# Input projections of a hybrid decoder layer: TensorE in written order, the forget gates one product on, x in natural order

## The chip, the cores and the metric

The kernel runs on one core of a Trainium2 chip (trn2). The metric is the device time of one execution in microseconds. A core has five engines with instruction streams of their own: TensorE (PE in the profile; PEld is its weight load), VectorE (DVE), ScalarE (ACT), GpSimd (POOL) and SyncE (SP). Each works through its stream in order, and they wait for each other by semaphores. SP and ACT also issue transfers (their DMA queues). TensorE writes to PSUM, which the other engines must empty before a bank can be written again.

## The reference

One layer of a causal decoder over S = 2048 tokens of D = 1024 channels, in float32:

```python
nx = rmsnorm(h, attn_norm_g[l])
proj = jnp.einsum('bsd,dp->bsp', nx, w_in[l])
gq, gk, gv, gr, glow, dq, dk_, dv_ = jnp.split(proj, split_at, axis=-1)

gate_pre = (jnp.einsum('bsr,rk->bsk', glow, gla_gate_w2[l]) + gla_gate_b[l]).astype(jnp.float32)
glog = jax.nn.log_sigmoid(gate_pre) / GLA_TAU
o_a = gla_mixer(gq, gk, gv, glog)                  # reshaped per head
...
o_b = dilated_mixer(dq, dk_, dv_, rel_bias)        # reshaped per head
...
h = h + jnp.einsum('bsm,md->bsd', mixed, w_out[l])
nm = rmsnorm(h, mlp_norm_g[l])
a = jnp.square(jax.nn.relu(jnp.einsum('bsd,df->bsf', nm, w_ff1[l])))
h = h + jnp.einsum('bsf,fd->bsd', a, w_ff2[l])
```

The case is about the first lines: the norm of x, the projection `nx @ w_in` (1024 to 3088 columns), the forget gate made from the 16 low-rank columns `glow`, and the tables of the relative-position bias that the dilated attention reads later.

## The kernel before

**Products.** Every float32 matrix product is made of three matmuls on split operands (`mm3`, L67 to L69): high part by high part, low by high, high by low. On top of this the projection uses a scheme with seven products instead of eight for each block of 2 by 2: the 1024 tokens of a half in two blocks, channels in two blocks, a group's columns in two blocks. The seven sums of the x blocks, transposed so that channels lie on the partitions, are kept in the tiles `tb1` to `tb7` (high and low); the seven sums of the weight blocks are made as they are needed by `prep(at)` (L202 to L214) out of `wraw` into a ring of three `wcomb` tiles, two jobs ahead.

**Groups and jobs.** The columns of `w_in` are cut into nine groups, in this order: dv, gr, four of dq and dk, gq, gk, gv. Each is done for the first 1024 tokens and then again for the second, which makes 18 groups; each group has seven jobs, one for each of the seven products, in the order 1, 2, 5, 6, 3, 4, 7. So there are 126 jobs, numbered from 0. A job of a wide group (dv, gr, gv: two blocks of 256 or 264 columns) consists of four products, one for each tile of 128 tokens, `product(at, i)`; a job of a narrow group is one product with 512 tokens as the moving side. Each product is twelve matmuls into one PSUM bank. The banks come from rings with the tags a (2 banks), c (3), d (2) and o (1); products take them in the turn a, c, a, o. Behind each product `rest()` moves it out of PSUM and into the sums of its group, on ACT, DVE and POOL (L300 to L321), and `finish` stores columns that are done.

**The gates.** The group gr holds the output gate (248 or 264 columns a block) and, at the end of its second block, the 16 columns `glow`. The second column block is finished, for both token blocks, by the seventh product, so that the last job of the group (job 13 in the first token half, job 76 in the second) ends with eight gates, two behind each of its four products: for the two token tiles t that the product completes. There `rest()` runs L317 (DVE, out of PSUM), L318 (POOL) and L319 (DVE), and then `finish` twice. For gr, `finish` takes the log-sigmoid (`log_sigmoid`, L125 to L128: Abs, Exp and Ln on ACT, one DVE instruction), an Exp (L260), a DVE product (L261) and a POOL product (L262), stores the block, and calls `gate`. `gate` transposes glow (16 columns, L227) into a bank d, copies it to a small tile `gT` (L228), multiplies it by `w2b` into another bank d (L230), and runs the log-sigmoid on 256 columns straight from that bank.

**x.** `x_load` fetches a tile of 128 tokens by `token_rows`, in an order in which partition p holds token (p div 8) + 16 (p mod 8) of the tile, so that tokens 16 apart lie together. A tile is squared and summed on ACT (`x_stat`, L358), scaled by its inverse root and by the gain row `gB` (L370), which one transfer has spread over all partitions, and transposed by `transposed` (L378) with the identity. The first eight tiles are done in the opening, jobs 0 to 4, which is written out by hand. The other eight come from `second_half`, a generator that is advanced at the jobs listed in `OTHER`: load, norm (L420, L93, L94, L422), two times eight transposes, sums and stores to DRAM, from where `reload` brings them back for the second token half.

**Biases.** At job 65 `bias_rows` loads a table and makes three rows by three matmuls (L334) into the one o bank, with a DVE copy behind each (L335), and stores them to `rowD`. `spread_bias` then repeats each row over 128 partitions by a transfer from DRAM to DRAM on ACT's queue (L341): twelve of them, written at every third job from 72 to 105.

**What sets the order.** Within `tc.manual_schedule(engines=...)` the engines named keep the order in which the instructions are written. Outside, a scheduler at build time orders each engine's stream, by a model of its own and by the data that each instruction needs. Before, only the opening (jobs 0 to 4) is manual, for TensorE, DVE, ACT and POOL; SP's stream is the scheduler's throughout, and so is all of the loop over jobs 5 to 125. There the twelve bias transfers stand together on ACT's queue, soon after the rows, and the gates stand between the products of the following jobs.

Of the kernel before, what the change touches and what calls it, by code (L numbers as in the profile page):

```python
# [41 lines left out]
def emit(tc, a, stop=99):  # L42
# [35 lines left out]
    make_identity(nc, ident)  # L78
    mhalf = const.tile([128, 4], F32, name="mhalf")
    V.memset(mhalf, -0.5)  # L80
    stats = const.tile([128, 96], F32, name="stats")
    stat_at = [0]

    def stat(n=1):
        if stat_at[0] + n > 96:
            stat_at[0] = 0
        s = stats[:, stat_at[0]:stat_at[0] + n]
        stat_at[0] += n
        return s
# [132 lines left out]
    def gate(glow, t):  # L222

        gT = gTs[t % 2]
        V.memset(gT, 1.0)
        pt = ps("d")
        T.transpose(pt[:16, :128], glow, ident)  # L227
        V.tensor_copy(gT[:16], pt[:16, :128])  # L228
        pg = ps("d")[:, :256]
        T.matmul(pg, gT, w2b, start=True, stop=True)  # L230
        e = stage()[:, :256]
        log_sigmoid(e, pg)
        SP.dma_start(glD[t * 128:t * 128 + 128], e)
# [39 lines left out]
    banks = [0]  # L273

    def product(at, i):
# [11 lines left out]
        else:  # L287
            p = p[:, :w]
            tk = slice(i * 128, i * 128 + 128)
            for c in range(4):  # L290
                mm3(p, B[0][:, c, tk], B[1][:, c, tk], W[0][:, c], W[1][:, c], c == 0, c == 3)

# [32 lines left out]
    def bias_rows():  # L325
# [5 lines left out]
        SP.dma_start(oh, a["c_onehot"])  # L331
        for d in range(3):
            p = ps("o")
            T.matmul(p[:8, :384], rb, oh[:, d], start=True, stop=True)  # L334
            V.tensor_copy(rbo[:, d], p[:8, :384])  # L335
        SP.dma_start(rowD, rbo)

    def spread_bias(d, h):

        row = rowD[h:, d]  # L340
        A.dma_start(rbD[d][h:h + 2].rearrange("h p n -> p h n"),  # L341
                    bass.AP(tensor=row.tensor, offset=row.offset, ap=[[0, 128], [3 * 384, 2], [1, 384]]))
# [5 lines left out]
    def x_load(t, dst):  # L348
        SP.dma_start(dst, token_rows(x2, t, D))
# [22 lines left out]
    def transposed(xt, last=None):  # L372
        out = []
        for q in range(2):
            pv = view(ps("cd"[q]), (4, 128))
            for k in range(4):
                of = xt[:, (4 * q + k) * 128:(4 * q + k + 1) * 128]
                T.transpose(pv[:, k, :], last if last is not None and 4 * q + k == 7 else of, ident)  # L378
# [6 lines left out]
    def first_half(t):  # L385

        pv = transposed(xs[t])
# [22 lines left out]
    def second_half():  # L410

        b = [view(bp[:, 512 * q:], (4, 128)) for q in range(4)]
        for i in range(4):
# [10 lines left out]
            for k in range(2):  # L424
                for q, pv in enumerate(transposed(xp[:, D * k:])):
# [16 lines left out]
    with tc.manual_schedule(engines={nc.tensor.engine, nc.vector.engine, nc.scalar.engine, nc.gpsimd.engine}):  # L442
        x_load(0, xs[0])
        SP.dma_start(gB, bcast_row(a["attn_norm_g"], D))
# [55 lines left out]
    other, back = second_half(), []  # L500
    for at in range(5, len(jobs)):
# [13 lines left out]
        if at == 7 * NG + 2:  # L515
            bias_rows()
        if 7 * NG + 8 <= at < 7 * NG + 44 and at % 3 == 0:
            spread_bias(2 - (at - 7 * NG - 8) // 12, (at - 7 * NG - 8) // 3 % 4 * 2)
    if stop <= 1:
# [872 lines left out]
```

## Time and profile before

| what | value |
|---|---|
| median of three runs | 2397.13 us (2396.92 to 2399.54) |
| the profiled execution, device time | 2398.99 us |
| its span, as the profile has it | 2397.2 us, 1.8 less than its device time |
| granted TensorE clock over the span | 0.985 |
| opening (jobs 0 to 4) | 0 to 73 us |
| loop over jobs 5 to 125 | 73 to 582 us |
| attention, output projection and feed-forward | 582 us to the end |

The profile is of one execution. PE, PEld, DVE, ACT and POOL are the busy times of the engines, with the number of their instructions. A row of a group of instructions has the line, the engine, the operation, output and input with their shapes, the count, then the busy time in us and the mean of one in ns, and at last the idle time of the engine just before them with what ended it. A row of the timeline has the start, the duration, and in brackets the idle time of its engine before it. A row of windows has the stretch, its length, and for each engine busy time and count, then the granted clock of TensorE (1 is full), the mean busy share of the 16 DMA engines and GB/s. Durations of successive matmuls overlap, since they are pipelined: the matmuls of 264 columns last 0.28 us each and start 0.12 us apart. The chain that ended last is followed back from the last instruction, at each step to what released it.

### The profile page before, as it was taken

To read this page: it belongs to the slowest core of one execution; us is meant where nothing else is said; L and a number is where in the kernel's file an instruction comes from. 1 tells how busy PE (TensorE), PEld (TensorE's weight loads), DVE (VectorE), ACT (ScalarE), POOL (GpSimd) and SP (SyncE) were. 2 spreads that over 40 slices of the span, in tenths; PEclk is the share of its full clock that TensorE was granted. 3 is DMA by queue.
4 is the path that set the end of the run, shared out by engine and by line. 5 is a ranking of instruction groups with operands and counts; after the bars stand their busy time and mean duration, and the time that the engine had idled before them with its cause. 6 is when DMAs were issued, how large, how long until landed. Compare 5 with 4: busy or idle time off the path is not lost.

```text
span 2397.2 us, 35124 instructions
## 1 busy us (share of the span) xinstructions
PE 2306.6 (96%) x12648; PEld 1989.9 (83%) x12648; DVE 1561.9 (65%) x2879; ACT 1148.0 (48%) x2181; POOL 583.3 (24%) x551
## 2 busy tenths in 40 slices
PE   6999998999999989999999999999999999999998
PEld 5877898779989988888788887888888888888886
DVE  6878666765667668445677778877773455556555
ACT  5565434533767657223455556555563333224323
POOL 5555435446566665100000000000000100001002
PEclk9999999999999999999999999999999999999999
DMA  6457664757888867468664447544467496457653
GB/s 159 120 164 230 213 189 136 206 166 194 213 193 226 225 174 241 154 201 267 203 206 145 145 149 242 176 162 157 155 203 274 155 315 208 168 170 248 217 167 106
DMA packets 342540, 458.13 MB, mean 191 GB/s; under 512 B 19620, under 2 KB 215733, under 8 KB 336094
## 3 DMA queue, kind: packets, MB, share of 16 engines
q1 hardware_dynamic: 313614, 413.15, 56.0%
q10 hardware_dynamic: 28752, 42.74, 5.2%
q8 instruction: 99, 1.62, 0.3%
q14 instruction: 75, 0.61, 0.1%
HBM read 293.51 MB, written 167.02 MB: 192 GB/s over the span
## 4 chain that ended last, share of the span: by engine, by line
PE 77%; DMA 8%; DVE 7%; issue 3%; ACT 3%; POOL 1%; SPq 1%; ACTq 0%; POOLq 0%; DVEq 0%
PE ps_a L67 8%; PE ps_a L68 8%; PE ps_a L69 8%; PE ps_c L67 7%; PE ps_c L69 7%; PE ps_c L68 7%; PE ps_d L67 4%; PE ps_d L69 4%; PE ps_d L68 4%; PE ps_a L672 4%; PE ps_o L67 3%; PE ps_o L68 3%; PE ps_o L69 3%; PE ps_d L653 2%; DMA cmb<-boD 2%
## 5 line engine op out<-in xcount | busy, mean ns | idle before, releaser
L1226 POOL TENSOR_TENSOR suma<-suma,gs 128x512 f32<-128x512 f32 x16 | 23.3, 1472 | 1152.6 <-ACT scr L1224 1152.5
L346 DVE TENSOR_TENSOR ca<-ra,ca 128x1024 fp32r<-128x1024 f32 x112 | 137.7, 1230 | 164.4 <-ACT ca L345 164.4
L345 ACT ACTIVATE ca<-ra 128x1024 fp32r<-128x1024 f32 x112 | 118.0, 1054 | 225.8 <-PE ps_c L69 185.4
L345 ACT ACTIVATE w1comb<-w1raw 128x512 fp32r<-128x512 f32 x224 | 139.6, 627 | 158.7 <-PE ps_c L69 57.7
L644 ACT ACTIVATE pe<-pe,O 128x256 f32<-128x256 f32 (+1 forms) x384 | 157.6, 454 | 89.1 <-DVE O L643 76.3
L672 PE MATMUL ps_a<-v,pt 128*128 128x65 f32 x1200 | 185.1, 258 | 13.3 <-DVE pt L662 8.5
L672 PEld LDWEIGHTS ps_a<-v,pt 128*128 128x128 f32 x1200 | 180.9, 200 | 16.1 <-DVE pt L662 9.5
L346 DVE TENSOR_TENSOR w1comb<-w1raw,w1comb 128x512 fp32r<-128x512 f32 x224 | 153.6, 689 | 53.4 <-ACT w1comb L345 53.2
L653 PE MATMUL ps_d<-ident,pe 128*128 128x128 f32 x600 | 160.9, 284 | 0.0
L643 DVE CUSTOM_DVE_ANT_0 pe<-ps_c,nb 128x256 f32<-128x256 f32 (+1 forms) x384 | 126.6, 360 | 43.4 <-PE ps_d L653 20.6
L204 DVE TENSOR_TENSOR wcomb<-wraw,wcomb 128x512 fp32r<-128x512 f32 (+2 forms) x84 | 101.2, 1210 | 70.3 <-ACT wcomb L202 68.8
L202 ACT ACTIVATE wcomb<-wraw 128x512 fp32r<-128x512 f32 (+2 forms) x126 | 96.3, 773 | 103.7 <-PE ps_a L69 20.8
L345 ACT ACTIVATE cb<-rb 128x1024 fp32r<-128x1024 f32 x56 | 59.4, 1061 | 158.0 <-PE ps_o L68 108.1
L67 PE MATMUL ps_c<-hb,w1comb 128*128 128x512 f32 x336 | 132.2, 393 | 2.8 <-ACT hb L345 2.8
L68 PE MATMUL ps_c<-hb,w1comb 128*128 128x512 f32 x336 | 132.2, 393 | 1.6 <-DVE w1comb L346 1.6
L69 PE MATMUL ps_c<-hb,w1comb 128*128 128x512 f32 x336 | 131.8, 392 | 0.0
L67 PE MATMUL ps_c<-cb,ca 128*128 128x512 f32 x336 | 130.8, 389 | 0.0
L68 PE MATMUL ps_c<-cb,ca 128*128 128x512 f32 x336 | 130.8, 389 | 0.0
L69 PE MATMUL ps_c<-cb,ca 128*128 128x512 f32 x336 | 130.8, 389 | 0.0
L653 PEld LDWEIGHTS ps_d<-ident,pe 128*128 128x128 f32 x600 | 111.1, 190 | 0.4
L94 POOL TENSOR_TENSOR stats<-stats,mhalf 128x1 f32<-128x1 f32 (+1 forms) x64 | 46.4, 730 | 259.3 <-DVE stats L93 216.1
L346 DVE TENSOR_TENSOR cb<-rb,cb 128x1024 fp32r<-128x1024 f32 x56 | 68.2, 1221 | 62.5 <-ACT cb L345 62.3
(351 smaller groups left out, 7330.2 us busy)
## 6 DMA issues: line engine op xcount, KB each, us to landing
ra<-actD SPq DMA_DIRECT2D x56, 1024.0 KB, 6.8
actD<-acc SPq DMA_DIRECT2D x192, 256.0 KB, 2.3
rb<-w_ff SPq DMA_DIRECT2D x72, 512.0 KB, 4.8
w1raw<-w_ff SPq DMA_DIRECT2D x32, 1024.0 KB, 7.3
k<-kD SPq DMA_DIRECT2D x32, 512.0 KB, 11.5
rb<-hTD SPq DMA_DIRECT2D x14, 1024.0 KB, 5.9
wraw<-w_in SPq DMA_DIRECT2D x48, 256.0 KB, 3.4
boD<-O SPq DMA_DIRECT2D x8, 1056.0 KB, 6.2
```

Source lines behind the costliest of these rows:

```text
L67: T.matmul(out, sh, mh, start=first, stop=False)
L68: T.matmul(out, sl, mh, start=False, stop=False)
L69: T.matmul(out, sh, ml, start=False, stop=last)
L94: G.tensor_tensor(r2, r, mhalf[:, :n], op=OP.pow)
L202: A.activation(hi, src, AF.Copy, scale=sc)
L204: V.tensor_tensor(lo, src, hi.bitcast(F32), op=OP.subtract)
L345: A.activation(hi, src, AF.Copy)
L346: V.tensor_tensor(lo, src, hi.bitcast(F32), op=OP.subtract)
L643: V.tensor_tensor_reduce(p, s, bias, scale=1.0, scalar=BIG, op0=OP.add, op1=OP.min, accum_out=nm)
L644: A.activation(p, p, AF.Exp, bias=nm, scale=-1.0)
L653: T.transpose(pb[:, i * 128:i * 128 + 128], src, ident)
L672: T.matmul(self.b.opsum[:, n % 4], self.pt[:, i * 128:i * 128 + 128], self.b.v[:, blk, cols], start=first, stop=last)
```

## The change

The whole loop over the jobs now runs with TensorE in written order; ACT, DVE, POOL and SP are still the scheduler's. Within a gate, what follows the copy to `gT` is put off in a list `waiting` and done behind the matmuls of the next product. x is loaded in natural order, and the transposes take a permutation matrix `perm` in place of the identity, which gives the same `tb` tiles. The gain row is loaded as a single row (4 KB, ACT's queue) and spread over the partitions by two matmuls against a row of ones, with two ACT copies, in place of a spreading transfer on SP's queue. The bias table is loaded at job 63 and its three matmuls come at job 66. The twelve transfers of `spread_bias` are pinned to their place in the written order. The ring of small statistics has 48 columns in place of 96. In the changed kernel's build the transfers of the GLA norm's gain (`gnB`), w2 and the gate's bias also stand further ahead on SP's queue, right behind the loads of x tiles 0 and 1.

```diff
@@ -76,13 +76,18 @@
     A.preload_act_table_set("natural_log_exp_and_others")
     ident = const.tile([128, 128], F32, name="ident")
     make_identity(nc, ident)
+
+    perm = const.tile([128, 128], F32, name="perm")
+    G.memset(perm, 0.0)
+    G.affine_select(out=perm, in_=perm, compare_op=OP.not_equal, fill=1.0, base=0, pattern=[[-1, 16], [-16, 8]],
+                    channel_multiplier=1)
     mhalf = const.tile([128, 4], F32, name="mhalf")
     V.memset(mhalf, -0.5)
-    stats = const.tile([128, 96], F32, name="stats")
+    stats = const.tile([128, 48], F32, name="stats")
     stat_at = [0]
 
     def stat(n=1):
-        if stat_at[0] + n > 96:
+        if stat_at[0] + n > 48:
             stat_at[0] = 0
         s = stats[:, stat_at[0]:stat_at[0] + n]
         stat_at[0] += n
@@ -221,16 +226,20 @@
 
     def gate(glow, t):
 
-        gT = gTs[t % 2]
+        gT = gTs[t // 4 % 2]
         V.memset(gT, 1.0)
         pt = ps("d")
         T.transpose(pt[:16, :128], glow, ident)
         V.tensor_copy(gT[:16], pt[:16, :128])
-        pg = ps("d")[:, :256]
-        T.matmul(pg, gT, w2b, start=True, stop=True)
-        e = stage()[:, :256]
-        log_sigmoid(e, pg)
-        SP.dma_start(glD[t * 128:t * 128 + 128], e)
+
+        def rest():
+            pg = ps("d")[:, :256]
+            T.matmul(pg, gT, w2b, start=True, stop=True)
+            e = stage()[:, :256]
+            log_sigmoid(e, pg)
+            SP.dma_start(glD[t * 128:t * 128 + 128], e)
+
+        waiting.append(rest)
 
     def finish(g, n, k, i):
 
@@ -270,7 +279,7 @@
         if kind == "dv":
             q.dma_start(token_rows(vN[:, j:], t, 512, w), s)
 
-    banks = [0]
+    banks, waiting = [0], []
 
     def product(at, i):
 
@@ -289,6 +298,8 @@
             tk = slice(i * 128, i * 128 + 128)
             for c in range(4):
                 mm3(p, B[0][:, c, tk], B[1][:, c, tk], W[0][:, c], W[1][:, c], c == 0, c == 3)
+        while waiting:
+            waiting.pop(0)()
 
         def rest():
             X, c11, c12, c21, c22 = [v[:, i * n:i * n + n] for v in (CX, *C[0], *C[1])]
@@ -329,6 +340,7 @@
         V.memset(rb[32:33], NEG)
         V.tensor_scalar(rb[:32], rb[:32], -1.0, None, op0=OP.mult)
         SP.dma_start(oh, a["c_onehot"])
+        yield
         for d in range(3):
             p = ps("o")
             T.matmul(p[:8, :384], rb, oh[:, d], start=True, stop=True)
@@ -338,15 +350,16 @@
     def spread_bias(d, h):
 
         row = rowD[h:, d]
-        A.dma_start(rbD[d][h:h + 2].rearrange("h p n -> p h n"),
-                    bass.AP(tensor=row.tensor, offset=row.offset, ap=[[0, 128], [3 * 384, 2], [1, 384]]))
+        tc.keep_in_program_order(A.dma_start(
+            rbD[d][h:h + 2].rearrange("h p n -> p h n"),
+            bass.AP(tensor=row.tensor, offset=row.offset, ap=[[0, 128], [3 * 384, 2], [1, 384]])))
 
     def split(hi, lo, src):
         A.activation(hi, src, AF.Copy)
         V.tensor_tensor(lo, src, hi.bitcast(F32), op=OP.subtract)
 
     def x_load(t, dst):
-        SP.dma_start(dst, token_rows(x2, t, D))
+        SP.dma_start(dst, x2[t * 128:t * 128 + 128])
 
     X = {}
 
@@ -369,13 +382,13 @@
         for cs in (slice(0, 512), slice(512, D)) if t == 0 else (slice(0, D),):
             V.scalar_tensor_tensor(xs[t][:, cs], x_src(t)[:, cs], X[t], gB[:, cs], op0=OP.mult, op1=OP.mult)
 
-    def transposed(xt, last=None):
+    def transposed(xt, last=None, by=ident):
         out = []
         for q in range(2):
             pv = view(ps("cd"[q]), (4, 128))
             for k in range(4):
                 of = xt[:, (4 * q + k) * 128:(4 * q + k + 1) * 128]
-                T.transpose(pv[:, k, :], last if last is not None and 4 * q + k == 7 else of, ident)
+                T.transpose(pv[:, k, :], last if last is not None and 4 * q + k == 7 else of, by)
             out.append(pv)
         return out
 
@@ -384,7 +397,7 @@
 
     def first_half(t):
 
-        pv = transposed(xs[t])
+        pv = transposed(xs[t], by=perm)
         i = t % 4
         b11, b21 = [view(xs[i][:, 512 * q:], (4, 128)) for q in range(2)]
         if t < 4:
@@ -422,7 +435,7 @@
                 V.scalar_tensor_tensor(xt, xt, r, gB, op0=OP.mult, op1=OP.mult)
             yield
             for k in range(2):
-                for q, pv in enumerate(transposed(xp[:, D * k:])):
+                for q, pv in enumerate(transposed(xp[:, D * k:], by=perm)):
                     A.activation(b[2 * k + q], pv, AF.Copy)
                 yield
             (b11, b21, b12, b22), (t2, t4, t3) = b, [view(xp[:, 512 * q:], (4, 128)) for q in range(3)]
@@ -441,7 +454,13 @@
 
     with tc.manual_schedule(engines={nc.tensor.engine, nc.vector.engine, nc.scalar.engine, nc.gpsimd.engine}):
         x_load(0, xs[0])
-        SP.dma_start(gB, bcast_row(a["attn_norm_g"], D))
+        g1, one = c11[:1, :D], CX[:1, :128]
+        A.dma_start(g1, a["attn_norm_g"])
+        V.memset(one, 1.0)
+        for q in range(2):
+            p = ps("a")
+            T.matmul(p, one, g1[:, 512 * q:512 * q + 512], start=True, stop=True)
+            A.activation(gB[:, 512 * q:512 * q + 512], p, AF.Copy)
         load_w(0, 0, 0)
         x_load(1, xs[1])
         load_w(0, 0, 1)
@@ -497,8 +516,9 @@
         for i in range(4):
             last_sums(i)
     prep(6)
-    other, back = second_half(), []
-    for at in range(5, len(jobs)):
+    other, back, rows = second_half(), [], bias_rows()
+
+    def job(at):
         g = jobs[at][0]
         if at + 2 > 6:
             prep(at + 2)
@@ -512,10 +532,14 @@
                 back.append(reload(order[at + 2 - 7 * NG + 7]))
         if at in OTHER:
             next(other)
-        if at == 7 * NG + 2:
-            bias_rows()
+        if at in (7 * NG, 7 * NG + 3):
+            next(rows, None)
         if 7 * NG + 8 <= at < 7 * NG + 44 and at % 3 == 0:
             spread_bias(2 - (at - 7 * NG - 8) // 12, (at - 7 * NG - 8) // 3 % 4 * 2)
+
+    with tc.manual_schedule(engines={nc.tensor.engine}):
+        for at in range(5, len(jobs)):
+            job(at)
     if stop <= 1:
         es.close()
         return
```

## The prediction

> **What bounds the kernel now.** I read the busy times first, then the slices, then the chain that ended last, then the first fifth of the span stretch by stretch.
>
> ```profile
> span 2397.2 us, 35124 instructions
> PE 2306.6 (96%) x12648; PEld 1989.9 (83%) x12648; DVE 1561.9 (65%) x2879; ACT 1148.0 (48%) x2181; POOL 583.3 (24%) x551
> PE   6999998999999989999999999999999999999998
> PE 77%; DMA 8%; DVE 7%; issue 3%; ACT 3%; POOL 1%; SPq 1%; ACTq 0%; POOLq 0%; DVEq 0%
> ```
>
> TensorE is busy 96% of the span and carries 77% of the chain. The change leaves its arithmetic alone but for two small matmuls, so it can win or lose only TensorE's idle time and the clock granted to it. The change touches the projections (0 to 582 us); split into opening and loop, each row giving length, then busy time of PE, PEld, DVE, ACT and POOL, clock and DMA share:
>
> ```profile
> 0.00:73.00 73.00, 48.30 (x310) 43.98 (x311) 49.38 (x66) 41.50 (x71) 37.65 (x31) 0.93 0.52 138
> 73.00:582.00 509.00, 479.87 (x2899) 417.77 (x2899) 355.41 (x478) 237.61 (x466) 259.29 (x191) 0.99 0.61 181
> ```
>
> TensorE is idle 73.00 − 48.30 = 24.7 us in the opening and 509.00 − 479.87 = 29.1 us in the loop. What it waited for longest in the loop (total, times, longest):
>
> ```profile
> PE ps_o L67 <- ACT acc L315: 5.8, 1, 5.8
> PE ps_c L378 <- DVE stats L93: 2.7, 1, 2.7
> PE ps_o L67 <- DVE acc L304: 2.4, 2, 1.5
> PE ps_d L378 <- DVE stats L93: 2.1, 1, 2.1
> PE ps_a L67 <- ACT acc L302: 2.1, 1, 2.1
> PE ps_c L67 <- ACT wcomb L202: 1.5, 1, 1.5
> ```
>
> Stalls cost more than their length: around three of them the granted clock (the figure behind the five busy times) fell.
>
> ```profile
> 137.00:139.50 2.50, 1.01 (x3) 0.65 (x4) 2.39 (x6) 2.47 (x7) 2.07 (x3) 0.99 0.16 54
> 139.50:143.00 3.50, 3.50 (x10) 2.68 (x10) 3.50 (x4) 2.39 (x7) 3.50 (x3) 0.52 0.28 73
> 214.50:218.00 3.50, 3.50 (x13) 3.12 (x14) 3.50 (x6) 2.65 (x6) 2.75 (x2) 0.51 0.52 187
> 368.00:371.50 3.50, 3.50 (x16) 3.50 (x17) 2.52 (x3) 0.95 (x1) 1.88 (x1) 0.50 0.94 268
> ```
>
> 3.5 us at half clock do half the work: one cooling costs about 1.7 us.
>
> **Gates in TensorE's program order.** Nothing on TensorE is added here; the order is. Before, the scheduler spread the eight gates of a group over many later products. After the second token half's job of the gate group (its last job, four products 0 to 3, two gates each) they stand so: product 0, transposes of its two gates, product 1, matmuls of those two gates, transposes of the next two, product 2, and so on; the last two matmuls come behind the next group's first product. "One product on" holds for the matmul alone. Two waits then stand bare. The transposes right behind a product need its evacuation: L317 and L319 on DVE, L318 on POOL. And there are two d banks: transposes take both, the two matmuls take both, and the next two transposes can start only when L128 on DVE has read both gate products, after Abs, Exp, Ln on ACT. No product stands between.
>
> ```profile
> 408.00:430.00 22.00, 22.00 (x116) 17.76 (x115) 18.90 (x35) 16.75 (x44) 13.82 (x15) 1.00 0.33 99
> L317 DVE TENSOR_TENSOR acc<-ps_a,acc x2: 429/431/433, 408.7 to 411.9; 128x264 f32<-128x264 f32 x2
> L125 ACT ACTIVATE acc<-ps_d 128x256 f32<-128x256 f32 x7 | 2.6, 376 | 0.1
> L126 ACT ACTIVATE acc<-acc 128x256 f32<-128x256 f32 x7 | 2.9, 416 | 0.1
> L128 DVE SCALAR_TENSOR_TENSOR acc<-ps_d,acc 128x256 f32<-128x256 f32 x7 | 2.8, 406 | 0.0
> L318 POOL TENSOR_TENSOR acc<-acc 128x264 f32<-128x264 f32 x4 | 3.6, 909 | 2.4 <-DVE acc L317 1.1 <-ACT acc L260 0.8 <-ACT acc L125 0.5
> L262 POOL TENSOR_TENSOR acc<-acc,misc 128x248 f32<-128x248 f32 x6 | 5.6, 934 | 3.6 <-DVE acc L261 3.6
> L230 PE MATMUL ps_d<-misc 17*128 17x256 f32 x16 | 5.6, 427 | 0.0
> L68 PE MATMUL ps_a<-tb,wcomb 128*128 128x512 f32 x36 | 14.6, 404 | 0.6 <-DVE wcomb L204 0.6
> 129.61 0.39 ACT L126 ACTIVATE acc<-acc 128x248 f32<-128x248 f32 x1
> 129.91 0.40 ACT L127 ACTIVATE acc<-acc 128x248 f32<-128x248 f32 x1
> ```
>
> Now TensorE has no idle in 408 to 430, where the second gate group's job falls. The walk after, for that group, with the changed program's order on DVE, ACT and POOL: behind product 0, L317 0.43 + L318 0.91 + hand-overs, 1.5 us. Behind the first two matmuls, six ACT passes at 0.30 us apart (129.61 to 129.91) plus L128 0.41 plus hand-overs, 2.4; some other passes stand between them, 2.7. For the third pair POOL has four L262 of the earlier tiles queued ahead of L318: 4 × 0.93 + 0.91 = 4.6, plus hand-overs 4.9. For the fourth two L262 and L318, 2.8, behind a DVE that is late by about one: 4.0. Together 13.1 us of idle, two coolings of 1.7, less the 0.6 of the L68 row, which goes: +16.0.
>
> The first group also has two x tiles in ACT's way:
>
> ```profile
> 125.57 0.28 PE L69 MATMUL ps_a<-wcomb,tb 128*128 128x264 f32 x1
> 137.00:170.00 33.00, 29.70 (x118) 21.33 (x118) 27.80 (x47) 23.59 (x56) 21.30 (x18) 0.95 0.43 131
> 133.07 1.06 ACT L420 ACTIVATE bp<-xp 128x1024 f32<-128x1024 f32 x1 [2.77 <-DMA xp<-x]
> 135.72 1.06 ACT L420 ACTIVATE bp<-xp 128x1024 f32<-128x1024 f32 x1 [0.89 <-DMA xp<-x]
> ```
>
> In the changed order the second L420 stands ahead of the second gate's Abs, so the log-sigmoids of the first pair wait for a tile that lands at 135.7; product 0 ended at 125.9, the first pair's matmuls would be through near 130 (1.5 wait, transposes 0.5, product 1.5, matmuls 0.7), the log-sigmoid near 139.4 (135.72 + 1.06 + three passes and L128), so the wait grows from 2.7 to about 9.4, with 1.4 more behind it: 13.1 + 8.1 = 21.2, plus 3.5 of cooling, less the 33.00 − 29.70 = 3.3 of idle that 137 to 170 us have now and their cooling of 1.7: +19.7. Both groups: **+35.7**. The floor is an order in which only the forced waits stay, 1.5 + 3 × 2.4 = 8.7 per group without cooling: 17.4 − 0.6 − 3.3 − 1.7 = +11.8. The ceiling stretches each shared DVE and POOL step by a third: +45. I take the walk, since the order of the queues is known and only durations are lent.
>
> **Biases.** Twelve ACT-queue transfers, before issued close together from 349.26 on, are pinned at every third job; the loads come three jobs before the three matmuls.
>
> ```profile
> 349.26 1.92 ACTq L341 DMA_DIRECT2D rbD<-rowD  x3
> 367.54 0.38 ACT L315 ACTIVATE acc<-ps_o 128x256 f32<-128x256 f32 x1 [11.79 <-DMA rbD<-rowD]
> 377.23 1.08 ACT L202 ACTIVATE wcomb<-wraw 128x1056 fp32r<-128x1056 f32 x1 [8.29 <-DMA vN<-acc]
> 341.59 0.81 PE L334 MATMUL ps_o<-xp 33*8 33x384 f32 x2
> ```
>
> ACT stood 11.8 us behind the transfers and TensorE 5.8 behind ACT; L202 was late at 377 for the same queue, 1.5. Both go, with the cooling of 368: −(5.8 + 1.5 + 1.7) = −9.0. The three L334 now come in a row, two of them behind a copy out of the one o bank: 2 × 0.85 = +1.7. What is late next: each pinned transfer stands on ACT's queue ahead of the q and k stores of the same jobs; +3, between 0 and +10 (one L315-sized wait of 5.8 with cooling, and some).
>
> **Waits for the normalised x tiles.** The transposes (L378) now stand four jobs behind the normalisation: 2.7 + 2.1 and the cooling of 214.5 go, −6.5; the other end is 0, if the norm is late there too.
>
> **Opening.** The gain row came by a broadcast transfer of 512 KB; now 4 KB, two fp32 matmuls and two ACT copies make it, ahead of the first Square.
>
> ```profile
> 1.49 5.53 DMA misc<-attn_norm_g
> 7.03 16.39 DMA acc<-x
> 5.86 1.06 ACT L358 ACTIVATE tb<-xp 128x1024 fp32r<-128x1024 f32 x1 [3.86 <-DMA xp<-x]
> 12.95 0.58 ACT L395 ACTIVATE xp<-ps_c 128x512 f32<-128x512 f32 x1
> 23.50 1.06 ACT L358 ACTIVATE tb<-acc 128x1024 fp32r<-128x1024 f32 x1 [4.26 <-DMA acc<-x]
> ```
>
> The matmuls cost 0.81 × 512 / 384 = 1.1 each at full clock and twice that cold, the copies 0.58 each: the first Square starts up to 3.4 later than 5.86. But ACT waits 4.26 for tile 4 at 23.50, which swallows it; that tile has 256 KB less ahead of it (512 KB gone, 256 KB of gnB brought forward), 1 to 2 us at the opening's 138 GB/s. Net +0.5, between −1.5 (tile 4 sets it) and +3.4 (nothing swallows it). The natural-order x loads and the other transpose matrix change neither count nor size of instructions: 0. Constants, a memset: 0, hidden by the wait of 3.86 ahead of the first Square.
>
> **Lost filling.** The scheduler put other products into waits for weight sums; program order can't. It still left such waits, the 2.1 at L302 and the 1.5 at L202 among them. +1, between 0 and +5. Behind 582 us the order hardly differs: 0.
>
> **Sum.** 35.7 − 9.0 + 1.7 + 3 − 6.5 + 0.5 + 1 = +26.4 on the profiled execution's 2399.0 (1.9 above the median): 2425; on the median 2423. Forecast **2424**.
>
> The Trainium skill's "TensorE: Matmul & The Clock Gate", Part 1 on the HAM clock gate, says the clock falls after an idle window of about 3.4 us, so that shorter gaps are harmless. The row of 137.00 shows 1.5 us idle out of 2.5 and the next row clock 0.52, so the trace disagrees. By the page, an estimate: half of the new coolings and the old ones at 139.5 and 214.5 drop out of the account, and the sum stays within some 4 us of the above.
>
> **The rivals.**
> 1. About the same: the gates cost only the floor, the rest as above. 26.4 − 35.7 + 11.8 = +2.5 on the median, 2400. For it: DVE (355 of 509 us) and ACT (238) have slack over the loop. Against: the L262 queued on POOL.
> 2. Faster: program order empties every stall that a late hoist caused, and the gates stay at their floor. TensorE's other idle in the loop beyond what is counted, 29.1 − 0.6 − 3.3 − 7.3 − 4.8 = 13.1, goes for its larger part, 9: 2.5 − 9 = −6.5, 2391. It decides where the idle of a gate group stays under 9 us. For it: the 2.4 at L304 and 2.1 at L302 are such stalls. Against: the two d banks force the log-sigmoid between two pairs whatever the order.
> 3. Slower still: the pinned transfers sit before q and k stores, the next evacuation into that tile waits, and ACT's queue is behind at each of twelve places, about 2 us each less the 3 counted: +20, 2444. For it: 11.8 us in one such queue. Against: two repeats of every third job are short beside three jobs.
> 4. The gates are as forecast but the bias cluster stays, since the transfers go on waiting for their row: +9, 2433.
>
> **How the numbers follow.** Chances: forecast 0.46, rival 1 0.13, rival 2 0.17, rival 3 0.16, rival 4 0.08. 0.2% is 4.8 us, about what tells this kernel from no change. Faster: rival 2 and a little of rival 1, 0.19. Same: most of rival 1 and the forecast's low edge, 0.13. Slower: 0.68. The range must reach rival 2 in part and rival 3: 2391 to 2445. The forecast's own: 2412 to 2435.
>
> **What would show it.** In the changed profile: TensorE idle at the transposes (L232) and the first matmul behind them, near 128 to 150 and 410 to 430 us, 21 and 13 us in all, released by DVE's log-sigmoid and POOL's L318; no wait at the L315 of 367; none at L378 for stats; twelve single bias transfers; the first Square at 7 to 9 us but tile 4 near 23. I am wrong if the idle per gate group is under 9 us, or if the opening moves by more than 4.

## The result and the profile after

The changed kernel takes 2428.89 us (median of 4 runs, 2428.55 to 2430.97), the kernel before on the same chip 2397.03; the ratio is 1.0135, 95% interval 1.012 to 1.0149. 2424 us were forecast. First the page of the changed kernel (span, busy times):

```profile
span 2426.4 us, 35168 instructions
PE 2319.1 (96%) x12652; PEld 2000.8 (82%) x12652; DVE 1565.5 (65%) x2880; ACT 1147.5 (47%) x2183; POOL 579.8 (24%) x553
```

The span grew by 29.2 us, TensorE's busy time by 12.5. TensorE does the same work but for the two small matmuls of the gain row, so most of that growth is put down to work done at a lower clock; two stretches alone account for some 9 us, below. Windows of the changed kernel: its opening ends near 69.3 us and its loop near 609.7 (length, busy times of PE, PEld, DVE, ACT and POOL, then clock, DMA share, GB/s).

```profile
0.00:69.30 69.30, 49.58 (x312) 43.67 (x313) 51.15 (x67) 42.60 (x73) 38.15 (x33) 0.98 0.41 138
69.30:609.70 540.40, 491.76 (x2901) 432.27 (x2900) 353.18 (x478) 236.56 (x466) 254.17 (x191) 0.95 0.57 171
```

The opening is 3.7 us shorter. The loop is 31.4 us longer: its idle rose from 29.1 to 540.40 − 491.76 = 48.6 us, its clock fell from 0.99 to 0.95. The waits of TensorE in the loop (total, times, longest) say where the idle is:

```profile
PE ps_d L232 <- DVE acc L133: 17.6, 6, 5.7
PE ps_a L67 <- ACT wcomb L207: 6.6, 4, 2.2
PE ps_a L67 <- ACT acc L313: 5.3, 3, 3.3
PE ps_d L232 <- POOL acc L329: 4.3, 2, 2.8
...
PE ps_a L68 <- DVE wcomb L211: 3.3, 3, 1.7
...
PE ps_d L232 <- DVE misc L233: 1.5, 4, 0.4
```

L232 is the gate's transpose, L133 the last step of the log-sigmoid, L329 the POOL sum of an evacuation (lines L227, L128 and L318 of the kernel before). Half of the idle, 17.6 + 4.3 + 1.5 = 23.4 us, stands at the gates' transposes. The wait of 5.8 at an evacuation by ACT near 368 us is gone, and so are those at the x transposes; the waits for weight sums have grown, from 8.5 us in all (L202, L204 and L206 before) to 14.3 (L207, L209 and L211). The gates one by one, in the timeline of TensorE (in brackets the idle time):

```profile
126.71 0.39 PE L232 MATMUL ps_d<-ident,acc 128*16 128x128 f32 x2 [2.75 <-POOL acc L329]
...
135.34 0.62 PE L232 MATMUL ps_d<-ident,acc 128*16 128x128 f32 x2 [5.72 <-DVE acc L133]
...
142.39 0.27 PE L232 MATMUL ps_d<-ident,acc 128*16 128x128 f32 x1 [2.37 <-DVE acc L133]
...
149.79 0.37 PE L232 MATMUL ps_d<-ident,acc 128*16 128x128 f32 x1 [2.60 <-DVE acc L133]
...
422.52 0.39 PE L232 MATMUL ps_d<-ident,acc 128*16 128x128 f32 x2 [1.59 <-POOL acc L329]
...
427.81 0.52 PE L232 MATMUL ps_d<-ident,acc 128*16 128x128 f32 x2 [2.37 <-DVE acc L133]
...
433.56 0.37 PE L232 MATMUL ps_d<-ident,acc 128*16 128x128 f32 x1 [2.72 <-DVE acc L133]
...
441.11 0.37 PE L232 MATMUL ps_d<-ident,acc 128*16 128x128 f32 x1 [1.79 <-DVE acc L133]
```

In each group the first pair waits for the evacuation, and the three others for the log-sigmoid that holds the d banks. Windows over these stretches show the second price:

```profile
135.00:155.00 20.00, 13.90 (x52) 10.72 (x53) 10.99 (x33) 11.07 (x34) 9.76 (x11) 0.72 0.31 98
434.00:447.00 13.00, 10.53 (x32) 7.78 (x32) 6.83 (x20) 6.58 (x20) 6.88 (x7) 0.52 0.33 102
```

The clock stood at 0.72 and 0.52 there; busy time by what is missing of the clock, 13.90 × 0.28 + 10.53 × 0.48, makes 9.0 us, an estimate from the mean clock of each window.

To see all stretches on one scale, I take the start of the first instruction that moves a job's first product out of PSUM, and subtract its start in the kernel before. The offsets, in us (negative is earlier), for the changed kernel and for the experiments told below, each from its one profiled execution. That execution can lie off the median (e3's 6.1 us below it, e9's 3.5 below, e10's 3.8 above), and the seven kernels that share the changed opening scatter from −3.4 to −5.1 at job 7, so differences of 1 to 2 us between rows mean little:

| kernel | job 7 | 13 | 21 | 63 | 76 | 84 | 125 | median, us | ratio to before, 95% |
|---|---|---|---|---|---|---|---|---|---|
| changed | −4.3 | −2.3 | 10.9 | 14.5 | 12.3 | 27.5 | 27.7 | 2428.9 | 1.012 to 1.0149 |
| e1 | −5.0 | −3.9 | −3.8 | −3.3 | −13.1 | −13.8 | −8.9 | 2390.7 | 0.9962 to 0.9981 |
| e2 | −4.8 | −2.3 | 7.3 | 12.4 | 9.4 | 18.9 | 19.0 | 2418.7 | 1.0078 to 1.0108 |
| e3 | −3.8 | −2.4 | 5.5 | 8.9 | 6.8 | 19.4 | 20.3 | 2422.5 | 1.0087 to 1.0119 |
| e4 | 0.5 | 0.1 | 24.0 | 30.6 | 37.5 | 62.2 | 57.5 | 2456.3 | 1.0229 to 1.0263 |
| e5 | −1.8 | −2.1 | −2.2 | −2.9 | −3.6 | −3.6 | −2.2 | 2394.5 | 0.9973 to 1.0006 |
| e6 | −6.5 | −4.1 | −6.1 | −5.6 | −4.5 | −4.5 | −4.8 | 2391.8 | 0.9965 to 0.9994 |
| e7 | −5.1 | −4.6 | 8.0 | 6.0 | 4.6 | 19.9 | 20.0 | 2413.6 | 1.0045 to 1.009 |
| e8 | −5.0 | −2.9 | −2.8 | −0.6 | −3.9 | −4.7 | −4.4 | 2392.8 | 0.9962 to 0.9994 |
| e9 | −3.4 | −1.1 | −0.5 | 2.3 | −0.5 | −1.7 | 3.4 | 2401.8 | 1.0008 to 1.0035 |
| e10 | −6.5 | −4.3 | −5.4 | −3.0 | −12.9 | −14.0 | −10.2 | 2388.2 | 0.9938 to 0.9968 |
| e12 | −7.4 | −8.4 | −11.1 | −13.1 | −22.7 | −23.9 | −20.0 | 2377.8 | 0.9895 to 0.9934 |
| e13 | −7.4 | −8.5 | −12.4 | −9.6 | −19.1 | −19.5 | −12.3 | 2382.3 | 0.9915 to 0.9949 |

For the changed kernel: opening −4.3, jobs 7 to 13 +2.0, first gate group (13 to 21) +13.2, 21 to 63 +3.6, the biases (63 to 76) −2.2, second gate group (76 to 84) +15.2, 84 to 125 +0.2, behind the loop +1.5, whose cause is open.

These stretches don't separate the terms cleanly. In the kernel before, the gate products (L230) run on to 189.3 and 467.9 us, and at jobs 21 and 84 four of a group's eight gates were still ahead, some 0.96 us of TensorE each (0.69 for the product, 0.27 for the transpose). So up to some 4 us of a group's figure come back later: at job 91 the offset is 24.0, which leaves 11.7 for the second group. The stretch behind the first group is then too low by as much.

### The profile page after: what moved, and what is told of

Read it like the earlier page. It is cut to its first block, busy times and chain, and to the rows that moved or that the text cites. A ratio compares the mean times of both kernels' runs of the same rounds, so it can differ in the third digit from the quotient of the medians.

```text
span 2426.4 us, 35168 instructions
## 1 busy us (share of the span) xinstructions
PE 2319.1 (96%) x12652; PEld 2000.8 (82%) x12652; DVE 1565.5 (65%) x2880; ACT 1147.5 (47%) x2183; POOL 579.8 (24%) x553
## 4 chain that ended last, share of the span: by engine, by line
PE 71%; DMA 4%; DVE 4%; ACT 2%; issue 1%; SPq 0%; ACTq 0%; POOL 0%; POOLq 0%; DVEq 0%
PE ps_a L68 7%; PE ps_a L69 7%; PE ps_a L67 7%; PE ps_c L67 6%; PE ps_c L68 6%; PE ps_c L69 6%; PE ps_d L67 4%; PE ps_d L68 4%; PE ps_d L69 4%; PE ps_a L696 4%; PE ps_o L67 2%; PE ps_o L68 2%; PE ps_o L69 2%; PE ps_d L677 2%; PE ps_c L655 2%; PE ps_c L657 2%
## 5 line engine op out<-in xcount | busy, mean ns | idle before, releaser
L207 ACT ACTIVATE wcomb<-wraw 128x512 fp32r<-128x512 f32 (+2 forms) x126 | 96.3, 774 | 140.9 <-PE ps_a L69 31.3
L667 DVE CUSTOM_DVE_ANT_0 pe<-ps_c,nb 128x256 f32<-128x256 f32 (+1 forms) x384 | 126.5, 360 | 42.1 <-PE ps_d L677 17.6
L209 DVE TENSOR_TENSOR wcomb<-wraw,wcomb 128x512 fp32r<-128x512 f32 (+2 forms) x84 | 98.6, 1182 | 74.2 <-ACT wcomb L207 74.0
L67 PE MATMUL ps_a<-wcomb,tb 128*128 128x256 f32 (+1 forms) x336 | 99.9, 297 | 10.0 <-ACT acc L313 5.3
## 6 DMA issues: line engine op xcount, KB each, us to landing
k<-kD SPq DMA_DIRECT2D x32, 512.0 KB, 11.7
```

The costliest lines, as they stand in the source:

```text
L67: T.matmul(out, sh, mh, start=first, stop=False)
L207: A.activation(hi, src, AF.Copy, scale=sc)
L209: V.tensor_tensor(lo, src, hi.bitcast(F32), op=OP.subtract)
L667: V.tensor_tensor_reduce(p, s, bias, scale=1.0, scalar=BIG, op0=OP.add, op1=OP.min, accum_out=nm)
```

## The experiments

### Is the loss TensorE's written order, and which part of it?

**e1**, the changed kernel with the loop left to the scheduler on TensorE:

```diff
-    with tc.manual_schedule(engines={nc.tensor.engine}):
-        for at in range(5, len(jobs)):
-            job(at)
+    for at in range(5, len(jobs)):
+        job(at)
```

> The changed kernel, but the loop over the jobs is left to the scheduler on TensorE again; gates put off, natural x, gain row, pinned repeats stay. Theory (the order of the gates on TensorE, with two d banks, is the loss; the rest of the change gains): 2385 to 2395 us, no idle at the gates' transposes beyond 3 us in all, opening still near 3.7 us earlier than before. Rival (the loss lies in pinned repeats, gain row or natural x): stays above 2415.

Measured 2390.7 us, as the theory had it. So the written order costs 38 us in the changed kernel, and everything else in the change together gains 6, with an interval that ends below 1. The gates' transposes kept one wait of 1.35.

**e4**, the converse: the kernel before with nothing but the written order.

```diff
-    for at in range(5, len(jobs)):
-        g = jobs[at][0]
+    with tc.manual_schedule(engines={nc.tensor.engine}):
+        for at in range(5, len(jobs)):
+            g = jobs[at][0]
...
```

> The kernel before, only with TensorE in written order over the loop; gates whole behind their own product, in one bank pair, repeats of biases left to the scheduler. Theory: eight gates a group one after the other, each with a transpose, copy, matmul and log-sigmoid in the two d banks, lose at least what the pairs lose, 23 us and cooling, and the gains of opening (3.7) and biases (2) are missing: 2430 to 2450 us. Rival (putting off by one product is itself the harm): 2400 to 2420.

Measured 2456.3 us, 6 above the upper end. The two gate groups (jobs 13 to 21 and 76 to 84) cost 23.9 and 24.7 us, against 13.2 and 15.2 with the gates' second part put off. The gates' waits in e4 are other ones than in the changed kernel:

```profile
PE ps_d L227 <- POOL acc L318: 17.9, 8, 5.2
PE ps_d L230 <- DVE misc L228: 10.6, 16, 1.6
```

With the gates whole, the transposes wait for POOL's part of the evacuation and the products for the copy, not for a log-sigmoid. Putting off is a remedy for the written order, and takes back some 20 of the 49 us that the two groups cost in e4 (which also lacks the rest of the change).

**e9**, the changed kernel with the written order everywhere but around the gates:

```diff
+    free = {*range(13, 24), *range(76, 87)}
...
+        if at in free:
+            job(at)
+            at += 1
+            continue
+        with tc.manual_schedule(engines={nc.tensor.engine}):
+            while at < len(jobs) and at not in free:
+                job(at)
+                at += 1
```

> The changed kernel with TensorE in written order, except for jobs 13 to 23 and 76 to 86, which the scheduler orders, so that the gates may stand between later products. Theory (the gates in written order cost 13 and 15 us, the written order elsewhere some 5 more net): the offset against the changed kernel at job 91 is some 27 us, 2400 to 2405. Rival (the written order of the other jobs is the larger loss): above 2412.

Measured 2401.8 us, inside. With the scheduler ordering 22 of the 121 jobs, 27 of the 38 us are back. The two gate groups now cost +0.6 and −1.2 instead of 13.2 and 15.2; at job 91 the offset lies 23.7 below the changed kernel's, where some 27 were expected. Most of the other 11 us of the written order is not at the gates: between jobs 63 and 76 e9 gains 2.8 us and e1 9.8.

### What do the gates wait for?

**e3**, the gate product in the ring of three c banks:

```diff
-            pg = ps("d")[:, :256]
+            pg = ps("c")[:, :256]
```

> The changed kernel with the gate product in the ring of three c banks, so that a transpose never waits for a log-sigmoid. Theory (two d banks force the log-sigmoid between two pairs): idle at the transposes falls to the evacuation's 1.6 to 2.7 us a pair, and what is left of the log-sigmoid wait moves to the matmuls, one product later: 10 to 14 us less idle, 2412 to 2418 us. Rival (evacuation and POOL's queue are the wait, the banks only come last by chance): within 4 us of 2429.

The waits of TensorE in this kernel:

```profile
PE ps_a L67 <- ACT wcomb L207: 8.8, 4, 2.7
PE ps_c L237 <- DVE acc L133: 7.6, 4, 3.4
PE ps_d L232 <- POOL acc L329: 5.8, 4, 2.8
```

No transpose waits for a log-sigmoid any more; 7.6 us of that wait have moved to the matmuls (L237). The gates' idle fell from 23.4 to some 13 us, as expected, but the time only to 2422.5 (2416.4 to 2423.6), 4 above the expected range and 6 below the changed kernel, so between theory and rival; the trace is of the 2416.4. The bank is the place where the wait shows; more than half of the idle stays with more banks.

**e2**, one gate a product instead of two:

```diff
+    def gate_step():
+
+        if back_half:
+            back_half.pop(0)()
+        late = waiting[1] or waiting[0]
+        if late:
+            first, rest = late.pop(0)
+            first()
+            back_half.append(rest)
...
-        while waiting:
-            waiting.pop(0)()
+        gate_step()
```

`first` is memset, transpose and copy; `rest` the product, log-sigmoid and store.

> The changed kernel with TensorE in written order, but one gate a product: behind each product the matmul of the gate whose transpose stood a product earlier, then the next gate's transpose, so that eight gates take nine products, and a log-sigmoid has a whole product to end in. Theory (waits of the pairs are the loss): the 23 us of idle at the gates' transposes fall under 3, and the time to 2397 to 2403 us (2428.9 less 23 and four to five coolings of 1.7). Rival (written order costs as much anywhere, for want of filling): above 2415, with the idle moved to weight sums and evacuations.

Measured 2418.7 us: the rival's time, but not its place. The idle at the gates fell only from 23.4 to some 18.6 us, and was not spread thin but collected into one long wait a group; TensorE's timeline in this kernel (L239 is the gate's product, L234 the transpose):

```profile
130.70 0.69 PE L239 MATMUL ps_d<-misc 17*128 17x256 f32 x2 [0.48 <-DVE misc L235]
...
142.34 0.38 PE L234 MATMUL ps_d<-ident,acc 128*16 128x128 f32 x1 [10.95 <-DVE acc L133]
...
430.00 0.38 PE L234 MATMUL ps_d<-ident,acc 128*16 128x128 f32 x1 [5.98 <-DVE acc L133]
```

The gate product of 130.70 had its log-sigmoid done eleven us later. DVE's timeline shows what it stood behind until 141.88:

```profile
136.60 1.72 DVE L446 SCALAR_TENSOR_TENSOR xp<-xp,stats,misc 128x1024 f32<-128x1024 f32 x1 [1.15 <-POOL stats L99]
138.25 3.71 DVE L133 SCALAR_TENSOR_TENSOR acc<-acc 128x248 f32<-128x248 f32 x3
141.88 0.41 DVE L133 SCALAR_TENSOR_TENSOR acc<-ps_d,acc 128x256 f32<-128x256 f32 x1
```

Ahead of it in the queue stood the scaling of an x tile and three log-sigmoids of the output gate. A whole product of room (the 2.7 us of a narrow job) is not enough when the job before has given ACT and DVE some 50 passes each, counted in the program, the gates' own among them. The scheduler, which is free to place a gate's matmul many jobs later, has the room: in the kernel before, the gate products of the second group stand from 418 to 468 us. A fixed lag of one product does not.

### The x tiles

**e7**, the Square of each later x tile pinned on ACT to where it is written:

```diff
-                A.activation(bp[:, :D], xt, AF.Square, accum_out=ss)
+                tc.keep_in_program_order(A.activation(bp[:, :D], xt, AF.Square, accum_out=ss))
```

The reason to try it stands in the changed kernel, in ACT's timeline and then in TensorE's:

```profile
192.21 0.63 ACT L207 ACTIVATE wcomb<-wraw 128x512 fp32r<-128x512 f32 x1
197.31 1.06 ACT L433 ACTIVATE bp<-xp 128x1024 f32<-128x1024 f32 x1 [4.47 <-DMA xp<-x]
...
199.01 1.06 ACT L433 ACTIVATE bp<-xp 128x1024 f32<-128x1024 f32 x1 [0.55 <-DMA xp<-x]
...
200.06 0.61 ACT L207 ACTIVATE wcomb<-wraw 128x512 fp32r<-128x512 f32 x1
```

```profile
200.73 0.79 PE L67 MATMUL ps_a<-tb,wcomb 128*128 128x512 f32 x1 [2.16 <-ACT wcomb L207]
202.93 0.80 PE L68 MATMUL ps_a<-tb,wcomb 128*128 128x512 f32 x1 [1.40 <-DVE wcomb L211]
...
247.30 0.50 PE L67 MATMUL ps_a<-tb,wcomb 128*128 128x512 f32 x1 [1.05 <-ACT wcomb L207]
249.51 0.79 PE L68 MATMUL ps_a<-tb,wcomb 128*128 128x512 f32 x1 [1.71 <-DVE wcomb L211]
```

ACT waits 4.47 us for a tile whose Square is written at job 32, some five jobs later, and the weight sum behind it makes TensorE stand.

> The changed kernel, only that the Square of each later x tile is pinned on ACT to its written place, four jobs behind its load, where the scheduler had put it as early as it took the tile to be there. Theory (the Square waits for its tile, and weight sums and the first group's log-sigmoids wait behind it on ACT): the 7 us of idle at weight sums near 200 and 248 us go, the first group's 5.7 us wait falls to the 2.4 of the second group; with coolings 10 to 14 us less, 2415 to 2419. Rival (weight sums are late for their own loads): within 4 us of 2429.

Measured 2413.6 us, 15 below the changed kernel and a little better than the theory's range. Its waits:

```profile
PE ps_d L232 <- DVE acc L133: 14.0, 6, 2.7
...
PE ps_c L391 <- DVE xp L435: 5.2, 3, 2.4
...
PE ps_a L67 <- ACT wcomb L207: 3.4, 2, 2.2
```

The waits for weight sums near 200 and 248 us are gone, the longest at the gates fell from 5.7 to 2.7, jobs 21 to 63 went from +3.6 to −2.0. Jobs 13 to 21 still cost 12.6 us, though. The pin has its own price: TensorE waits 5.2 us for scaled tiles at L391. And only 7.7 of the 16.6 us by which the two traces differ are there at job 125; the rest arises behind the loop, where the edit changes nothing, and its cause is open.

**e10** and **e12**, the same question where the scheduler orders TensorE. e10 is e1 with the gain row by its broadcast transfer again; e12 is e10 with the pin.

```diff
-        g1, one = c11[:1, :D], CX[:1, :128]
-        A.dma_start(g1, a["attn_norm_g"])
-        V.memset(one, 1.0)
-        for q in range(2):
-            p = ps("a")
-            T.matmul(p, one, g1[:, 512 * q:512 * q + 512], start=True, stop=True)
-            A.activation(gB[:, 512 * q:512 * q + 512], p, AF.Copy)
+        SP.dma_start(gB, bcast_row(a["attn_norm_g"], D))
```

> The changed kernel with TensorE left to the scheduler over the loop (2390.7 us), and the gain row by its broadcast transfer again; natural x, pinned repeats and the gates' second part put off stay. Theory (natural x alone brought job 7 forward by 6.5 us, with the gain row it was 4.9, so the two matmuls and copies ahead of the first Square cost 1 to 2): job 7 6 to 7 us earlier than before, 2387 to 2390. Rival (the two gain together): job 7 less than 4 us earlier, 2391 or more.

> The kernel with TensorE left to the scheduler and the gain row by broadcast, natural x and pinned repeats, and with the Square of each later x tile pinned on ACT to its written place. Theory (where TensorE's order is the scheduler's, the late Square is already filled with other products, and pinning it can only delay the transposes): 2387 to 2393, no clear gain. Rival (the Square holds up ACT in any order): 4 us and more below the kernel without the pin, 2383 to 2386.

e10: 2388.2 us, job 7 earlier by 6.5, as expected; its interval overlaps that of e1. e12: 2377.8 us, the rival's side and 5 below its range: the pin is worth 10 us there too, and the traces of the two differ by 9.8 at job 125. Waits of TensorE in e10, then in e12:

```profile
PE ps_a L67 <- DVE acc L315: 4.0, 3, 2.7
PE ps_c L391 <- DVE xp L435: 2.9, 2, 2.2
PE ps_d L391 <- DVE stats L98: 2.4, 1, 2.4
```

```profile
...
PE ps_a L67 <- DVE acc L315: 1.4, 2, 0.9
...
PE ps_c L391 <- DVE xp L435: 1.1, 1, 1.1
```

I had taken the late Square to be filled by other products. It isn't: the 2.7 us at an evacuation by DVE and the 2.4 at an x transpose went with the pin as well. e12 is the best kernel of this study, 0.8% below the one before and 2.1% below the changed one:

```profile
span 2375.3 us, 35134 instructions
PE 2302.9 (97%) x12648; PEld 1984.6 (84%) x12648; DVE 1554.4 (65%) x2879; ACT 1147.2 (48%) x2181; POOL 582.5 (25%) x553
```

**e13**, e12 with the gates whole behind their own product:

```diff
-        def rest():
-            pg = ps("d")[:, :256]
...
-        waiting.append(rest)
+        pg = ps("d")[:, :256]
+        T.matmul(pg, gT, w2b, start=True, stop=True)
...
-        while waiting:
-            waiting.pop(0)()
```

> The kernel of 2377.8 us (TensorE by the scheduler, broadcast gain row, natural x, pinned repeats, pinned Square), only with each gate written whole behind its own product again. In written order the putting off was worth 27 us (2456.3 against 2428.9, beside other differences). Theory (where the scheduler orders TensorE, it places gate products late in any case): within 3 us, 2375 to 2381. Rival (the putting off helps the scheduler's order too): 4 us and more above, 2382 to 2390.

Measured 2382.3 us (2381.2 to 2385.5), 4.5 above e12, but beside a kernel before that took 1.8 more there, and with ratios whose intervals overlap. It leans to the rival without settling it. The two traces differ by 7.7 us at job 125, and these arise in jobs 21 to 42 (4.5) and 91 to 105 (3.1), not at the gates; why there is open.

### The opening

**e5**, the gain row alone on the kernel before (the lines that e10 takes out); **e6**, natural x alone (with the smaller ring of statistics):

```diff
-        SP.dma_start(dst, token_rows(x2, t, D))
+        SP.dma_start(dst, x2[t * 128:t * 128 + 128])
...
-        pv = transposed(xs[t])
+        pv = transposed(xs[t], by=perm)
```

> The kernel before, only with the gain row spread by two matmuls and two ACT copies, which also brings the three small loads forward on SP's queue. Theory (it is this that makes the opening 3.7 us shorter, since the broadcast transfer of 512 KB no longer stands ahead of the x tiles): job 7 starts 3 to 5 us earlier than before. Rival (the natural-order loads do it): job 7 within 1 us of before.

> The kernel before, only with x in natural order and the permutation in the transposes (and the ring of statistics at 48 columns). Theory (the gain row makes the opening shorter): job 7 within 1 us of before, time within 4 us of 2397. Rival: job 7 3 to 5 us earlier.

Both expectations were the wrong way round. The gain row brings job 7 forward by 1.8 us and its time, 2394.5, can't be told from before; natural x brings it forward by 6.5, 2391.8 us. With both, job 7 is 3.4 to 5.1 earlier (seven kernels, 4.5 on average), with natural x and the broadcast 6.5 to 7.4 (e6, e10, e12, e13; 7.0 on average): once the tiles come sooner, the two matmuls and copies ahead of the first Square take some 2 to 3 us back. The first Square starts at 4.68 us in e10 and at 7.51 in the changed kernel. The transfers of x tiles 4 to 7 in the first 30 us (count, size, median us from issue to landing), before and in e6:

```profile
acc<-x SPq DMA_DIRECT2D x4, 512.0 KB, 14.7
```

```profile
acc<-x SPq DMA_DIRECT2D x4, 512.0 KB, 9.6
```

In e5 the same row has 15.1. Size, count and queue are the same in all three, and the order of the loads on SP's queue is the same before and in e6; only the order of the source rows differs. Before, neighbouring partitions read rows 64 KB apart, in natural order 4 KB. The Trainium skill's "DMA: Bandwidth & Descriptors", section on latency and other measured facts, has transfers slow down at row pitches that are large powers of two, measured from 512 KB up, with the cause inferred; the rows here go the same way at 64 KB. Whether it is that cause was not tried.

### The biases

**e8**, e1 with the twelve repeats not pinned:

```diff
-        tc.keep_in_program_order(A.dma_start(
-            rbD[d][h:h + 2].rearrange("h p n -> p h n"),
-            bass.AP(tensor=row.tensor, offset=row.offset, ap=[[0, 128], [3 * 384, 2], [1, 384]])))
+        A.dma_start(rbD[d][h:h + 2].rearrange("h p n -> p h n"),
+                    bass.AP(tensor=row.tensor, offset=row.offset, ap=[[0, 128], [3 * 384, 2], [1, 384]]))
```

> The changed kernel with TensorE left to the scheduler over the loop, and the twelve repeats of the biases not pinned. Against the same kernel with them pinned (2390.7 us, and 11 us gained between jobs 67 and 70). Theory (the twelve transfers in front of ACT's work cost 7 us of idle and a cooling): the wait of some 6 us near 365 us is back, 2397 to 2402. Rival (that wait went for another reason, the earlier rows or the stores of dv on the same queue): 2389 to 2393.

The wait is back, in TensorE's timeline:

```profile
373.22 0.59 PE L67 MATMUL ps_c<-wcomb,tb 128*128 128x264 f32 x1 [5.09 <-ACT wcomb L207]
```

So, where the scheduler orders TensorE, the pins do remove that wait. In ACT's timeline of e8 what stood right ahead of the weight sum is a run of stores of v, from 366.04 to 371.98; five repeats were issued at 352.46 to 356.26, ahead of those stores:

```profile
372.08 1.08 ACT L207 ACTIVATE wcomb<-wraw 128x1056 fp32r<-128x1056 f32 x1 [10.68 <-DMA vD<-acc]
```

Yet the time, 2392.8 us, is the rival's and not the theory's. Between jobs 63 and 76 e1 with the pins gains 9.8 us and e8 without them 3.3; at job 125 the two stand only 4.5 apart. e1 gave back 5.2 us between jobs 84 and 112 (−13.8 to −8.6), e8 0.8 (−4.7 to −3.9). The difference lies in the stretch of the pinned transfers and behind it; that these hold up q and k stores on ACT's queue was not shown one by one. And the pins don't empty that place in the written order. ACT's timeline of the changed kernel:

```profile
386.85 1.08 ACT L207 ACTIVATE wcomb<-wraw 128x1056 fp32r<-128x1056 f32 x1 [12.12 <-DMA vD<-acc]
```

ACT again stands 12 us before a weight sum, now behind eight pairs of stores of v (vD, vN) on its own queue, and TensorE's wait of 3.3 us at L313 near 388 comes from there.

## Why the prediction was right, and where it was not

The sign, the main mechanism (the gates in written order) and the size were right: 2424 forecast, 2428.9 measured, inside the forecast's own range of 2412 to 2435. The sum is better than its terms: +26.4 against +29.2 by the spans, with terms off by up to 10 us, both ways. That they cancel to within 3 us is luck.

| term | predicted | measured | from |
|---|---|---|---|
| gates, first group | +19.7 | +13.2 | jobs 13 to 21 |
| gates, second group | +16.0 | +15.2 | jobs 76 to 84 |
| x tiles' waits | −6.5 | +3.6 | jobs 21 to 63 |
| biases | −4.3 | −2.2 | jobs 63 to 76 |
| opening | +0.5 | −4.3 | job 7 |
| lost filling, and behind the loop | +1 | +3.7 | the rest |

**Gates.** The order was read rightly: evacuation first, then three waits for the log-sigmoid with no product between; e9 shows that these two places carry 27 of 38 us. Two sizes were off. The step "For the third pair POOL has four L262 of the earlier tiles queued ahead of L318", 4.9 us, and its like for the fourth, 4.0, did not come: the waits were 2.72 and 1.79 and ended by the log-sigmoid. POOL was through with two of the four at 427.98, just after TensorE's wait for the second pair, with the other two at 431.85, and with its evacuation at 432.55, one us before the log-sigmoid let the third pair go at 433.56. So the second group's idle, 1.59 + 2.37 + 2.72 + 1.79 and some small ones, 9.2 us, is nearly the floor of 8.7. In the first group the x tiles were in the way as predicted, but the Square began at 128.2 and not at 133.1, so that wait was 5.72 and not 9.4. Idle in all was 23.4 us against 34.3 worked out; the coolings cost 9.0 and not 7. Rival 1's condition on the idle was thus half met, without its time: its floor had no cooling in it, and it too had counted on the two terms that follow. The gate figures of the table hold up to some 4 us that belong to later stretches, as said above; the second group's 11.7 at job 91 is then below the 16.0, and not beside it.

**x tiles.** This is the step that failed: "The transposes (L378) now stand four jobs behind the normalisation: 2.7 + 2.1 and the cooling of 214.5 go, −6.5; the other end is 0". The measured +3.6 lies beyond that other end. The written order holds for TensorE alone. On ACT the scheduler still puts the Square where it takes the tile to be there, some five jobs early, and the wait that left the transposes went to the weight sums behind the Square (2.16 + 1.40 us near 200, 1.05 + 1.71 near 248). e7 shows it for these waits, and e12 that the early Square cost time in the scheduler's order too.

**Opening.** "The natural-order x loads and the other transpose matrix change neither count nor size of instructions: 0" was wrong: the loads land in 9.6 instead of 14.7 us and are the whole gain (e6). The row that said so was at hand, the 16.39 us of the chain for one tile of 512 KB. The price of the gain row, matmuls and copies ahead of the first Square, was of the right size, 2 to 3 us of the 3.4 that were its upper end. By the prediction's own sign, "if the opening moves by more than 4", the −4.3 at job 7 counts against it; and tile 4's Square, expected near 23 us, started at 18.26.

**Biases.** The 5.8 at L315 went as predicted, and a pinned transfer's cost of +3 later may have its like in the 5.2 us that e1 gives back between jobs 84 and 112, but in the changed kernel jobs 84 to 125 show only +0.2. What was missed is the next in line, the stores of v on the same queue.

**Rivals.** Rival 2 needed the idle of a gate group under 9 us and nine more us from elsewhere; the second group came to 9.2 and elsewhere gave nothing. Rival 3's +20 did not come. Rival 4's time, 2433, lies as near to 2428.9 as the forecast's 2424 does; what speaks against it is that the twelve repeats now stand singly, from 403.7 to 533.4 us, and that the wait of 5.8 is gone, though 3.3 us stayed near that place behind the stores of v.

## What to carry to other kernels

When one engine is taken out of a scheduler's hands, read the streams of the others for what stands ahead of each of its waits: a written order on TensorE only moves a wait if ACT still takes an early, not yet loaded tile first. Work that gives two engines fifty passes within four products needs a lag of many products, not of one; more banks (e3) or thinner slices (e2) brought back only 6 and 10 of the 38 us. A single pin on the instruction that waits for a transfer gained 10 us (e12 against e10) where the written order of a whole loop cost 38.

## What the runs showed of the hardware

The order of the source rows alone (e6 against before) made equal transfers of 512 KB land in 9.6 instead of 14.7 us. And TensorE's granted clock stayed low over 13.7 us although no single idle time from 427 to 447 us was longer than 2.72. It fell behind 3.4 us in which TensorE was busy for 1.44:

```profile
429.40:432.80 3.40, 1.44 (x8) 0.83 (x6) 2.01 (x7) 2.38 (x8) 2.42 (x3) 1.00 0.34 116
432.80:446.50 13.70, 10.40 (x31) 7.73 (x32) 7.67 (x21) 7.78 (x24) 6.88 (x7) 0.50 0.34 104
```

So this cooling outlasted the 3.5 us that the prediction counts for one from three rows of before. Two further waits of 0.37 us and one of 1.79 lie in the stretch; that they prolonged it is likely, but no run shows it. The Trainium skill's "TensorE: Matmul & The Clock Gate", Part 1 on the HAM clock gate, ties the fall to an idle window of about 3.4 us; the rows here disagree.
